# Row maxima of attention scores from 64-row products, neighbours on the lower and the upper half of the rows

## The chip, the core and the metric

The kernel runs on one core of one Trainium2 chip. A core has a matrix engine (TensorE, in the profile PE, its weight loads PEld), three engines for elementwise work (VectorE = DVE, ScalarE = ACT, GpSimd = POOL), a queue engine that issues DMAs (SyncE = SP), an on-chip memory with 128 rows (partitions), and eight banks in which TensorE leaves its results. The metric is the time of one execution on the device in microseconds (us).

## What is computed

A two-layer encoder over 1024 tokens of width 1024: an attention layer and a spatial gating layer, each followed by a squared-ReLU MLP, and a last RMSNorm. The change touches the attention layer alone. It has sixteen query heads of 64 channels. Eight (group A) look at a window of 128 tokens to either side, with one more logit per head; eight (group B) look at all tokens:

```
# group A, banded: s is masked outside |i - j| <= 128
m = jnp.maximum(jnp.max(s, axis=-1, keepdims=True), sink_b)
p = jnp.exp(s - m)
denom = jnp.sum(p, axis=-1, keepdims=True) + jnp.exp(sink_b - m)
# group B
s = jnp.einsum('bqhgd,bkhd->bhgqk', qblk.astype(jnp.float32), kf) * scale
p = jax.nn.softmax(s, axis=-1)
```

The row maximum m only shifts the exponent; any number near it gives the same p / denom. So it can be taken from a coarser product than the scores themselves.

## The kernel before, in words

Most products are made in three parts: each f32 operand is split into a high part, rounded to the format that TensorE takes in one pass (float32r), and a low part, the rest; the products high x high, high x low and low x high are added.

For the scores of a head, rows 0 to 63 and 64 to 127 of the on-chip memory are used for two parts at once. `load_head` brings the queries: R1 (tile r1, in listings r) holds the high part twice, in rows 0 to 63 and again in 64 to 127; R2 (r2) holds the low part in rows 0 to 63, and rows 64 to 127 later take the negated row maxima. `load_k` brings the keys of a key head: k1 holds the high part in rows 0 to 63 and the low part in rows 64 to 127; k2 holds the high part in rows 0 to 63 and ones in rows 64 to 127 (a memset on GpSimd). A score tile (st) is then k1 x R1 + k2 x R2, two products of 128 rows, shifted by the maxima already; group A has a third between them for the mask. ScalarE takes the exponent (pe, ea), and for group B the result is split again (pp, on ScalarE, VectorE and GpSimd) for the products with the values (av).

The maxima come ahead of that, from products of their own (tile mx): R1 x k1, that is q_high x (k_high + k_low), one product of 128 rows. `mx_units` makes the list of them for a head: for group B sixteen, two halves of 512 keys for each of eight blocks of 128 queries; for group A eight, with 256 or 384 keys each. VectorE reduces each to one column (mb for group B, mj and ma with mask and sink for group A). After four query blocks the columns are gathered (m), and `bcast` turns them on TensorE into a row for every partition (bc), which VectorE copies into rows 64 to 127 of R2.

The order around the change: `heads` runs b, b, a, a, b, a, b, a and so on. Each head has 16 units (b) or 8 (a); in a unit come a score tile, then as many mx as `mx_to` asks for, then the av products of the unit six back. `mx_to(count)` issues mx units until `count` of them have been issued in all, so that the maxima run two to two and a half heads ahead. The first ones stand in the last projection, whose products are named lin. A scheduler then lays down the order within each engine, and waits are added from it. All result tiles (st, mx, av, bc, lin) share the eight banks.

Of the kernel before, what the change touches and what calls it, by code (L numbers as in the profile page):

```python
# [13 lines left out]
P = 128  # L14
# [18 lines left out]
def tile_kernel(ctx: ExitStack, tc: tile.TileContext, I, out, upto=99, dbg=None):  # L33
    nc = tc.nc
    pe, act, dve, pool, sp = nc.tensor, nc.scalar, nc.vector, nc.gpsimd, nc.sync
# [11 lines left out]
    def nm(s):  # L47
        uid[0] += 1
        return f"{s}_{uid[0]}"

    def blk(s, dt=F32R):
        return blkp.tile([P, 2, HN], dt, tag="blk", name=nm(s))

    def tr(s, dt=F32):
        return trp.tile([P, HN], dt, tag="tr", name=nm(s))
# [4 lines left out]
    def sm(s, shape):  # L60
        return smp.tile(shape, F32, tag=s, name=nm(s))

    def ps(s):
        return psp.tile([P, HN], F32, tag="ps", name=nm(s))

    def f(ap):
        return ap.bitcast(F32)
# [3 lines left out]
    def mm(o, l, r, start, stop, **kw):  # L71
        last_mm[0] = pe.matmul(o, l, r, start=start, stop=stop, **kw)  # L72
# [396 lines left out]
    for half in range(2):  # L469
# [27 lines left out]
        for tb in range(4):  # L497
            sc = rc[:, tb : tb + 1]
            for kv in range(4):
                src = vp[tb // 2][:, tb % 2, kv * 64 : (kv + 1) * 64]  # L500
                hi = v1[kv][:, half * 4 + tb, 0:64]
# [32 lines left out]
    heads, seen = [], {"a": 0, "b": 0}  # L534
# [3 lines left out]
    k1, k2 = {}, {}  # L538
    R1, R2 = {}, {}
# [3 lines left out]
    def kv_of(hd):  # L543
        return (0 if hd[0] == "a" else 2) + hd[1] // 4

    def load_k(kv):
        a = blk("k1")
        b = blk("k2")
        hi, lo = (qs["k"][part, kv].rearrange("r n t -> (r n) t") for part in range(2))
        sp.dma_start(f(a[0:64].rearrange("p a b -> p (a b)")), hi)  # L550
        sp.dma_start(f(a[64:128].rearrange("p a b -> p (a b)")), lo)
        sp.dma_start(f(b[0:64].rearrange("p a b -> p (a b)")), hi)
        pool.memset(f(b[64:128]), 1.0)
        k1[kv] = a.rearrange("p a b -> p (a b)")
        k2[kv] = b.rearrange("p a b -> p (a b)")

    def load_head(n):
        hd = heads[n]
        kv = kv_of(hd)
        if kv not in k1:  # L560
            load_k(kv)
        key = f"{hd[0]}{hd[1] // 4}"
        assert all((q, half) in ready for q in (key, "k") for half in range(2))
        hi, lo = (qs[key][part, hd[1] % 4].rearrange("r n t -> (r n) t") for part in range(2))
        a, b = blk("r1"), blk("r2")
        a = a.rearrange("p a b -> p (a b)")
        b = b.rearrange("p a b -> p (a b)")
        sp.dma_start(f(a[0:64]), hi)
        sp.dma_start(f(a[64:128]), hi)
        sp.dma_start(f(b[0:64]), lo)  # L570
        R1[n], R2[n] = a, b


    def mx_units(n):
        hd = heads[n]
        kv = kv_of(hd)
        if hd[0] == "a":
            M[n] = sm("ma", [P, 8])

            def unit(tb):  # L580
                lo, hi = max(tb - 1, 0), min(tb + 2, 8)
                w_ = (hi - lo) * P
                off = (lo - tb + 1) * P
                p_ = ps("mx")[:, 0:w_]
                mm(p_, R1[n][:, tb * P : (tb + 1) * P], k1[kv][:, lo * P : hi * P], True, True)
                j = tr("mj")
                dve.tensor_tensor_reduce(
                    j[:, 0:w_], p_, maskq[:, off : off + w_], 1.0, sink8[:, hd[1] : hd[1] + 1],
                    ALU.add, ALU.max, M[n][:, tb : tb + 1],
                )  # L590
                if tb % 4 == 3:
                    m4 = smp.tile([P, 4], F32R, tag="m4", name=nm("m4"))
                    dve.tensor_copy(m4, M[n][:, tb - 3 : tb + 1])
                    chains.append(bcast(n, tb // 4, m4))

            return [lambda tb=tb: unit(tb) for tb in range(8)]
        M[n] = sm("mb", [P, 8, 2])

        def unit(tb, kh):
            p_ = ps("mx")  # L600
            ks = slice(kh * HN, (kh + 1) * HN)
            mm(p_, R1[n][:, tb * P : (tb + 1) * P], k1[kv][:, ks], True, True)
            dve.tensor_reduce(M[n][:, tb, kh : kh + 1], p_, axis=AX.X, op=ALU.max)  # L603
            if tb % 4 == 3 and kh == 1:
                m4 = smp.tile([P, 4], F32R, tag="m4", name=nm("m4"))
                dve.tensor_reduce(m4, M[n][:, tb - 3 : tb + 1, :], axis=AX.X, op=ALU.max)
                chains.append(bcast(n, tb // 4, m4))

        return [lambda tb=tb, kh=kh: unit(tb, kh) for tb in range(8) for kh in range(2)]

    def bcast(n, half, m4):
        for _ in range(2):
            yield 1
        p_ = ps("bc")
        for i in range(4):
            mm(p_[:, i * P : (i + 1) * P], m4[:, i : i + 1].to_broadcast([P, P]), identn, i == 0, i == 3)
        dve.tensor_copy(R2[n][64:128, half * HN : (half + 1) * HN], p_[64:128])
        shifted.add((n, half))
# [141 lines left out]
    def n_mx(n):  # L760
        return sum(8 if hd[0] == "a" else 16 for hd in heads[: max(n, 0)])

    def mx_to(count):

        while mxn[1] < min(count, n_mx(16)):
            if not mxq:
                mxq.extend(mx_units(mxn[0]))
                mxn[0] += 1
            mxq.pop(0)()
            mxn[1] += 1  # L770

    def qa_hook(half, k):
        if half == 1:
            if k == 1:
                load_to(2)
            if k >= 3:
                mx_to((k - 3 + 1) * 4)
# [5 lines left out]
    for n in range(16):  # L783
        if n > 0:
            load_to(n + 3)
        units = st_units(n)
        start, goal = mxn[1], n_mx(n + 2) + int((n_mx(n + 3) - n_mx(n + 2)) * 0.6)
        if n == 0:
            goal = n_mx(2)
        for i, u in enumerate(units):  # L790
            avs = u()
            mx_to(start + -(-(goal - start) * (i + 1) // len(units)))
            avq.append(avs)
            if len(avq) > LAG:
                for a in avq.pop(0):
                    a()
            tick()
        if n >= 13:
            ahead(base[3] + (n - 12))
# [558 lines left out]
```

## Time and profile before

| | |
|---|---|
| median of 3 runs | 2095.03 us (2094.3 to 2097.71) |
| profiled execution | 2097.54 us, its span in the trace 2095.8 us |
| TensorE busy | 2036.0 us, 97% of the span, 9126 products |
| weight loads busy | 1676.2 us, 80% |
| VectorE busy | 1459.8 us, 70% |
| ScalarE busy | 961.2 us, 46% |
| GpSimd busy | 564.0 us, 27% |
| mean granted clock of TensorE | 0.992 |

The span runs from the first to the last instruction of the trace. Products are pipelined: a product's busy time covers that of the next one in part, so its price when others follow is the distance between starts. Shares are means over stages that differ; the change lies in the attention stage, some 290 us of the span.

### The profile page before, as it was taken

Reading aid. Unit: us, or ns where it says so; the run is one execution under the profiler, and the core shown is the slowest. Engines: PE = TensorE matmul, PEld = TensorE weight load, DVE = VectorE, ACT = ScalarE, POOL = GpSimd, SP = SyncE. Lnnn points to the kernel's source line nnn. Section 1 sums busy time; section 2 is a strip of 40 time slices with the busy share of each in tenths; the row PEclk is TensorE's granted clock in tenths of the full one; section 3 lists DMA queues with packets and bytes.
Section 4 is the critical chain, followed back from the end, with each engine's and each line's share of the span. In section 5 each row is a group of like instructions: output and inputs, shape, how many; then the busy total and the mean of one; then the engine's idle time right before and its main releaser. Section 6 shows DMA issues by size and latency. Waiting matters only on the chain. (4 is left out here: it accounts for less than half of the span.)

```text
span 2095.8 us, 27079 instructions
## 1 busy us (share of the span) xinstructions
PE 2036.0 (97%) x9126; PEld 1676.2 (80%) x9126; DVE 1459.8 (70%) x2324; ACT 961.2 (46%) x1768; POOL 564.0 (27%) x437
## 2 busy tenths in 40 slices
PE   8998999999899999999999999999899999999997
PEld 7786877788688888888888888887788888888885
DVE  6878878856786666756696545556866667846975
ACT  5525677773433333435454434433433334544542
POOL 4325466543132222200002126322232223000021
PEclk9999999999999999999999999999999999999998
DMA  4364121134044444768464210432254446855542
GB/s 163 125 195 122 42 65 46 31 111 158 23 165 148 151 156 165 264 204 293 131 220 144 77 57 11 151 107 75 81 174 148 161 151 205 294 218 195 170 140 95
DMA packets 207307, 294.92 MB, mean 141 GB/s; under 512 B 19648, under 2 KB 88768, under 8 KB 207168
## 3 DMA queue, kind: packets, MB, share of 16 engines
q1 hardware_dynamic: 207168, 293.19, 42.5%
q8 instruction: 72, 1.18, 0.2%
q14 instruction: 67, 0.55, 0.1%
HBM read 207.13 MB, written 85.98 MB: 140 GB/s over the span
## 5 line engine op out<-in xcount | busy, mean ns | idle before, releaser
L72 PE MATMUL up<-h,w 128*128 128x512 f32 x1536 | 372.2, 395 | 18.6 <-ACT r L916 9.3
L72 PE MATMUL dy<-w,w 128*128 128x512 f32 x1536 | 364.7, 389 | 0.0
L72 PEld LDWEIGHTS up<-h,w 128*128 128x128 f32 x1536 | 292.9, 191 | 83.1 <-ACT r L916 10.1
L72 PEld LDWEIGHTS dy<-w,w 128*128 128x128 f32 x1536 | 288.3, 188 | 60.3 <-issue 0.5
L314 POOL TENSOR_TENSOR ss<-ss,sq 128x512 f32<-128x512 f32 x66 | 103.4, 1568 | 676.7 <-ACT sq L313 582.1
L72 PE MATMUL up<-w,w 128*128 128x512 f32 x1152 | 277.0, 390 | 0.0
L72 PE MATMUL dx<-w,w 128*128 128x512 f32 x1152 | 276.7, 389 | 0.0
L72 PEld LDWEIGHTS up<-w,w 128*128 128x128 f32 x1152 | 216.4, 188 | 46.0 <-issue 1.0
L72 PEld LDWEIGHTS dx<-w,w 128*128 128x128 f32 x1152 | 216.2, 188 | 44.9
L146 ACT CAST w<-wr 128x512 fp32r<-128x512 f32 x288 | 166.7, 620 | 136.9 <-DVE wr L179 37.3
L147 DVE TENSOR_TENSOR w<-wr,w 128x512 fp32r<-128x512 f32 x288 | 198.1, 699 | 24.2 <-ACT w L146 20.1
L72 PE MATMUL lin<-h,w 128*128 128x512 f32 x768 | 181.3, 393 | 1.1 <-POOL w L123 0.5
L72 PEld LDWEIGHTS lin<-h,w 128*128 128x128 f32 x768 | 143.3, 188 | 33.7 <-issue 2.4
L951 POOL TENSOR_TENSOR t<-ua,ub 128x512 f32<-128x512 f32 x32 | 43.9, 1371 | 459.8 <-ACT ua L898 422.9
L645 POOL TENSOR_TENSOR pp<-pe,pp 128x512 fp32r<-128x512 f32 x107 | 143.4, 1362 | 76.9 <-ACT pp L641 60.4
L147 DVE TENSOR_TENSOR w<-ur,w 128x512 fp32r<-128x512 f32 x224 | 156.0, 707 | 5.8 <-ACT w L146 5.6
L146 ACT CAST w<-ur 128x512 fp32r<-128x512 f32 x224 | 135.8, 620 | 42.3 <-DVE w L147 19.7
L147 DVE TENSOR_TENSOR w<-ws,w 128x512 fp32r<-128x512 f32 x128 | 94.0, 734 | 67.5 <-ACT w L146 67.0
L72 PE MATMUL st<-r,k 128*128 128x512 f32 (+2 forms) x384 | 131.0, 398 | 4.6 <-DVE mb L603 3.6
L146 ACT CAST w<-ws 128x512 fp32r<-128x512 f32 x128 | 79.5, 621 | 110.8 <-DVE ws L226 75.8
L898 ACT ACTIVATE ua<-ua 128x512 f32<-128x512 f32 x64 | 40.4, 633 | 179.0 <-DVE ua L897 179.0
L897 DVE SCALAR_TENSOR_TENSOR ua<-up,rstd 128x512 f32<-128x512 f32 x32 | 22.1, 690 | 139.5 <-PE up L72 139.5
(191 smaller groups left out, 3134.2 us busy)
## 6 DMA issues: line engine op xcount, KB each, us to landing
ur<-ucd SPq DMA_DIRECT2D x224, 256.0 KB, 3.6
wr<-in_w SPq DMA_DIRECT2D x256, 128.0 KB, 2.7
ucd<-t SPq DMA_DIRECT2D x128, 256.0 KB, 2.0
wr<-in_w SPq DMA_DIRECT2D x128, 256.0 KB, 3.5
ucd<-ub SPq DMA_DIRECT2D x64, 256.0 KB, 2.0
x<-in_xT SPq DMA_DIRECT2D x32, 256.0 KB, 4.6
xmd<-x SPq DMA_DIRECT2D x32, 256.0 KB, 2.1
ucd<-ua SPq DMA_DIRECT2D x32, 256.0 KB, 2.0
```

The costliest lines, as they stand in the source:

```text
L72: last_mm[0] = pe.matmul(o, l, r, start=start, stop=stop, **kw)
L146: act.copy(w[:, 0], src)
L147: dve.tensor_tensor(w[:, 1], src, f(w[:, 0]), op=ALU.subtract)
L314: pool.tensor_tensor(sumsq[half][:, 0:w_], sumsq[half][:, 0:w_], t, op=ALU.add)
L645: lo.tensor_tensor(pp[:, 1], e, f(pp[:, 0]), op=ALU.subtract)
L897: dve.scalar_tensor_tensor(dst, src, 0.0, r[half], op0=ALU.max, op1=ALU.mult)
L898: act.activation(dst, dst, AF.Square)
L951: pool.tensor_tensor(t3, ua[:, 1], ub[:, 1], op=ALU.subtract)
```

## The change

Each product for the maxima takes 64 rows in place of 128: q_high x k_high, without k_low. There are two places where it can be made. On rows 0 to 63 it is R1's lower half with k2, and on rows 64 to 127 R1's upper half with k1, for which the two parts of k1 change places. Group B uses the lower half for its first 512 keys and the upper for the second, group A the lower for even query blocks and the upper for odd ones. `mx_to` rounds its count up to an even number, so that products are issued in twos.

```diff
@@ load_k
-        sp.dma_start(f(a[0:64].rearrange("p a b -> p (a b)")), hi)
-        sp.dma_start(f(a[64:128].rearrange("p a b -> p (a b)")), lo)
+        sp.dma_start(f(a[0:64].rearrange("p a b -> p (a b)")), lo)
+        sp.dma_start(f(a[64:128].rearrange("p a b -> p (a b)")), hi)
         sp.dma_start(f(b[0:64].rearrange("p a b -> p (a b)")), hi)
         pool.memset(f(b[64:128]), 1.0)
@@ new
+    def mx_mm(p_, n, rows, tb, ks):
+        rs = slice(64 * rows, 64 * rows + 64)
+        mm(p_, R1[n][rs, tb * P : (tb + 1) * P], (k2, k1)[rows][kv_of(heads[n])][rs, ks], True, True)
+
@@ mx_units, group A
-                mm(p_, R1[n][:, tb * P : (tb + 1) * P], k1[kv][:, lo * P : hi * P], True, True)
+                mx_mm(p_, n, tb % 2, tb, slice(lo * P, hi * P))
@@ mx_units, group B
-            mm(p_, R1[n][:, tb * P : (tb + 1) * P], k1[kv][:, ks], True, True)
+            mx_mm(p_, n, kh, tb, ks)
@@ mx_to
+        count += count % 2
         while mxn[1] < min(count, n_mx(16)):
```

On TensorE, in a head of group B (its scores are st, its query tiles r_423 and r_424 before, r_424 and r_425 after), with the maxima of a later head (query tile r_503): k_221 is k1 and k_222 is k2. Before:

```order
L72 MATMUL st_2499<-r_423_2037,k_221_1336 128x512
L72 MATMUL st_2499<-r_424_2038,k_222_1337 128x512
L72 MATMUL mx_2507<-k_221_1336,r_503_2309 128x512
L72 MATMUL av_2426<-pp_2401,v_3_89 128x512
L72 MATMUL av_2426<-pp_2401,v_4_91 128x512
L72 MATMUL av_2426<-pp_2401,v_3_89 128x512
L72 MATMUL st_2513<-r_423_2037,k_221_1336 128x512
L72 MATMUL st_2513<-r_424_2038,k_222_1337 128x512
L72 MATMUL mx_2521<-k_221_1336,r_503_2309 128x512
L72 MATMUL av_2426<-pp_2420,v_3_89 128x512
```

And after:

```order
L72 MATMUL st_2513<-r_424_2043,k_221_1336 128x512
L72 MATMUL st_2513<-r_425_2044,k_222_1337 128x512
L72 MATMUL mx_2521<-k_222_1337,r_503_2309 128x512
L72 MATMUL mx_2524<-k_221_1336,r_503_2309 128x512
L72 MATMUL av_2426<-pp_2423,v_3_89 128x512
L72 MATMUL av_2426<-pp_2423,v_4_91 128x512
L72 MATMUL av_2426<-pp_2423,v_3_89 128x512
L72 MATMUL st_2532<-r_424_2043,k_221_1336 128x512
L72 MATMUL st_2532<-r_425_2044,k_222_1337 128x512
L72 MATMUL av_2426<-pp_2442,v_3_89 128x512
```

One mx in nearly every unit has become two in every second unit, one on k2 (rows 0 to 63) and one on k1 (rows 64 to 127). Before, the 192 products stood in 158 groups, 131 of them single; now in 97, of which 84 are pairs, three are fours, one is a three and nine are single.

On VectorE, at the end of a half head of the same maxima: mb are the maxima, m the gathered column that bcast on TensorE waits for, r the copy back of its result, pp a cast or a difference for the av products. Before:

```order
L645 TENSOR_TENSOR pp_2476<-pe_2474,pp_2476 128x512
L603 TENSOR_REDUCE mb_2388<-mx_2521 128x1
L643 CAST pp_2504<-pe_2502 128x512
L603 TENSOR_REDUCE mb_2388<-mx_2535 128x1
L606 TENSOR_REDUCE m_575_2538<-mb_2388 128x4
L603 TENSOR_REDUCE mb_2388<-mx_2553 128x1
L617 CAST r_504_2310<-bc_2573 64x512
```

And after (the lines are numbered 5 higher there):

```order
L650 TENSOR_TENSOR pp_2476<-pe_2474,pp_2476 128x512
L608 TENSOR_REDUCE mb_2388<-mx_2521 128x1
L648 CAST pp_2507<-pe_2505 128x512
L608 TENSOR_REDUCE mb_2388<-mx_2524 128x1
L611 TENSOR_REDUCE m_572_2527<-mb_2388 128x4
L608 TENSOR_REDUCE mb_2388<-mx_2553 128x1
L608 TENSOR_REDUCE mb_2388<-mx_2556 128x1
L622 CAST r_504_2310<-bc_2563 64x512
```

Two maxima of the next half, in place of one, now stand between the gathered column and the copy back. The reductions themselves are the same in number and size.

## Rows read from the trace of the kernel before

**Rows 1.** Busy us of PE, PEld, DVE, ACT, POOL (instructions); clock, DMA share, GB/s.

```profile
148.00:437.00 289.00, 271.53 (x1275) 221.52 (x1275) 239.84 (x433) 199.22 (x368) 157.37 (x120) 0.99 0.24 63
```

**Rows 2.** Waits of TensorE from 148 to 437 us: us, times, longest.

```profile
PE bc L72 <- DVE m L606: 4.1, 3, 1.4
PE st L72 <- DVE mb L603: 3.6, 5, 0.9
PE bc L72 <- DVE m L593: 2.5, 3, 1.1
...
PE av L72 <- DVE mb L603: 0.9, 1, 0.9
```

**Rows 3.** The same table as rows 1 by ten us, two stretches.

```profile
300.00:310.00 10.00, 9.23 (x45) 7.61 (x44) 8.85 (x16) 4.60 (x10) 5.74 (x5) 1.00 0.25 61
...
400.00:410.00 10.00, 7.67 (x33) 5.35 (x31) 9.87 (x14) 8.06 (x17) 6.71 (x5) 1.00 0.31 79
```

**Rows 4.** Instructions on tile mx (min/median/max ns), and groups by form (busy, mean ns).

```profile
L72 PEld LDWEIGHTS mx<-k,r x192: 186/188/193, 147.8 to 436.9; 128*128 128x128 f32 x192
L603 DVE TENSOR_REDUCE mb<-mx x128: 673/679/693, 148.5 to 417.6; 128x1 f32<-128x512 f32 x128
L587 DVE CUSTOM_DVE_ANT_0 mj<-mx,maskq,sink x64: 473/616/621, 197.6 to 438.2; 128x384 f32<-128x384 f32 x48, 128x256 f32<-128x256 f32 x16
...
L72 PE MATMUL mx<-k,r 128*128 128x512 f32 x128 | 46.7, 398 | 1.4 <-DVE r L617 0.7 <-DVE mb L603 0.4
L72 PE MATMUL av<-ea,v 128*128 128x384 f32 x64 | 25.4, 485 | 0.0
L72 PE MATMUL mx<-k,r 128*128 128x384 f32 x48 | 16.1, 338 | 0.0
L72 PE MATMUL mx<-k,r 128*128 128x256 f32 x16 | 4.5, 280 | 0.0
```

**Rows 5.** Timeline of TensorE's products in a B head: start, us, what.

```profile
323.16 0.62 PE L72 MATMUL st<-r,k 128*128 128x512 f32 x2
323.63 0.40 PE L72 MATMUL mx<-k,r 128*128 128x512 f32 x1
323.86 0.85 PE L72 MATMUL av<-pp,v 128*128 128x512 f32 x3
324.54 0.61 PE L72 MATMUL st<-r,k 128*128 128x512 f32 x2
```

**Rows 6.** The same timeline in an A head, 384 and 256 columns.

```profile
300.85 0.34 PE L72 MATMUL st<-maskk,identn 128*128 128x384 f32 x1
301.02 0.35 PE L72 MATMUL st<-r,k 128*128 128x384 f32 x1
...
308.00 0.28 PE L72 MATMUL st<-r,k 128*128 128x256 f32 x1
308.12 0.28 PE L72 MATMUL st<-maskk,identn 128*128 128x256 f32 x1
```

**Rows 7.** Timeline of the weight loads at the place of rows 5.

```profile
323.63 0.65 PEld L72 LDWEIGHTS av<-pp,v 128*128 128x128 f32 x3
```

**Rows 8.** An mx product after a wait, on the same timeline.

```profile
406.29 0.50 PE L72 MATMUL mx<-k,r 128*128 128x512 f32 x1
```

**Rows 9.** Timeline: f32 products (av from ea) beside others.

```profile
318.04 0.81 PE L72 MATMUL av<-ea,v 128*128 128x384 f32 x2
318.39 0.91 PE L72 MATMUL st<-r,k 128*128 128x512 f32 x2
319.14 1.03 PE L72 MATMUL av<-ea,v 128*128 128x384 f32 x4
```

**Rows 10.** Issue of the third K DMA, landing times of K, first mx weight load.

```profile
136.90 0.60 SPq L552 DMA_DIRECT2D k<-qs_k  x1
...
DMA to landing us min/median/max: 3.5/4.6/5.6
...
147.83 0.87 PEld L72 LDWEIGHTS mx<-k,r 128*128 128x128 f32 x4
```

## The prediction

> **What bounds the kernel now.** I read the stages first. The products whose maxima are taken, called mx, run from 148 to 437 us [rows 4], and in those 289 us TensorE is busy 271.5, VectorE 239.8, ScalarE 199.2 and GpSimd 157.4 [rows 1]; what follows has no mx. So 17.5 us of the stage are open on TensorE, and all other time there is matrix work back to back. The waits of TensorE in that stage come next. The three longest end with VectorE, and a fourth does: 4.1 + 3.6 + 2.5 + 0.9 = 11.1 us, for the maxima of a half head (m) or for a bank that a maximum (mb) still holds [rows 2]. Third, the shares by ten microseconds: in 15 of the 29 stretches from 150 to 440 us VectorE is at 8.8 of 10 or more, and TensorE idles in such stretches [rows 3]. So TensorE sets the time of nine tenths of the stage and more, with VectorE close behind it. [...]
>
> **What an mx product costs.** There are 192: 128 with 512 columns, 48 with 384, 16 with 256 [rows 4]. Their busy time (398 ns) overlaps the next product's, so the price is the distance of starts. Three av products that follow one another start at 323.86 and the next thing at 324.54, which is 0.227 us for 512 columns [rows 5]. For 384 columns the distance is 0.17 and for 256 it is 0.12 [rows 6]. The weight load of an mx takes 188 ns and lies beneath the product before it: the loads of the three av at 323.63 start with the mx product itself [rows 5, 7].
>
> **The change, part by part.** *The rows.* Each product reads 64 rows where it read 128. Its columns stay, and so do the outputs and the 128 + 64 reductions on VectorE (679 and 616 ns in the median) [rows 4]. A product alone saves nothing, as its time goes by columns. What can be saved is that two neighbours on different halves of the rows, writing to two banks, run at one time. By the order of the changed kernel the 192 products stand in 97 groups between other work: 52 pairs of 512 + 512 columns, three groups of four and one of three (59 such pairs together), 16 pairs of 384 + 384, 16 of 384 + 256, and nine single products.
>
> *The gain, from both sides.* No row shows a product on 64 rows. Below, the pair takes as long as two products, and the gain is nothing. Above, it takes as long as its longer product: 59 x 0.227 + 16 x 0.17 + 16 x 0.12 = 13.4 + 2.7 + 1.9 = 18.0 us. Two weight loads must also fit into the time of one pair. Products of 256 columns, each with a load of its own, start every 0.12 us [rows 6], so a pair can't go below 0.24, and the sum is 59 x 0.21 + 16 x 0.10 + 16 x 0.05 = 12.4 + 1.6 + 0.8 = 14.8. I take 16.5, between the two with overlap: the halves share neither rows nor a bank, and parts of TensorE that don't share anything do overlap in the rows, as the load beneath the product does. [...]
>
> *The switch.* Each of the 97 groups changes from 128 rows to 64 and back, 194 changes, and the trace has none. Below, a change is free. Above, TensorE lets the last product run out and then loads weights in the open. The run-out is 0.40 busy less 0.227, 0.17 us [rows 5]. The load in the open is what the first product after a wait takes more, 0.50 at 406.29 against 0.40: 0.10 us [rows 5, 8]. Together 0.27 a change, 52 us in all. The nearest rows of a change in how the array works are those between products in plain f32 (av from ea) and the others. An f32 product of 384 columns is busy 485 ns against 338 for an mx, so one more stream of columns, 0.15; two of them and two of 512 columns then need 2 x (0.17 + 0.15) + 2 x 0.227 = 1.09, and took 319.14 - 318.04 = 1.10 [rows 4, 9]. That leaves nothing for two changes. I take 0.02 a change, what two such stamps can hide: 3.9 us. The gain on TensorE is 16.5 - 3.9 = 12.6 us. It is gone when a change costs 16.5 / 194 = 0.085.
>
> *What VectorE lets through.* Half of the stretches have VectorE at 8.8 or more. There the stage can't shorten by much more than the 0.1 to 1.2 us of ten that VectorE has free [rows 3], against the 0.4 (12.6 in 289) that TensorE would save; in these I count half, in the others all. So three quarters of 12.6 arrive, 9.5 us.
>
> *Two at a time.* Rounding the count up issues at most one product earlier, never later. Two maxima now come at once, so a cast of pp that VectorE makes behind them is up to 0.68 us later; its av product runs six units after it, and a unit of st, st, mx, av, av, av takes 324.54 - 323.16 = 1.38 us [rows 5], which covers it. Were that cover gone, each such cast would cost the 0.68. The pair needs two free banks of eight at once. Where VectorE is behind, this wait grows: it is 3.6 + 0.9 us now [rows 2], and I leave it there and keep its doubling for a rival.
>
> *The K load.* The products on the lower half now need the third of the three DMAs of a key head, not only the first two. It is issued at 136.90 and a landing takes at most 5.6 us, so 142.5; the first mx loads its weights at 147.83 [rows 10]. For the other heads the query loads come behind it on the same queue, and mx waited for these already. So it costs nothing. Without the 5 us of cover the first pair would stand 0.6 us, the distance of one DMA's issue. Which part of k1 holds the high or the low half changes no sum.
>
> *The sum.* Profiled execution 2097.54 us, span 2095.8 in it: less 9.5 is 2088.0. The profile lies 2.5 above the median of the runs, 2095.03, so there I forecast 2085.5, 0.45% less. About 0.2% (4.2 us) is what a measurement of this kernel tells from no change.
>
> **The rivals.** *The array must run empty at each change* (slower). Place: both edges of each of the 97 groups. Price: 0.27 by the rows above, 52.4 - 16.5 = 36 us more, of which up to 11.1 us fall into the waits for VectorE that are there now: 2120 to 2131. It turns the forecast's sign from 0.085 a change. For it speaks that a load in the open has a price in the rows, and that no row shows a load for 64 rows beneath a product of 128; against it that the f32 change leaves no gap. [...]
> *Only the load stands open*: 0.10 x 194 = 19.4, less 16.5, so 3 us more, 2098, of which the waits may take most: 2095 to 2099.
> *The two halves run one after the other* and a change is free: the change then does not do what it can do, and only the order differs: 2095, give or take 3.
> *VectorE takes the gain*: the bank waits double (4.5 us more) and the 9.5 shrink to 5: 2090.
>
> **How the numbers follow.** I give the forecast 0.40, VectorE taking half 0.07, the open load alone 0.13, one after the other 0.13, the empty array 0.27. Faster by over 0.2%: 0.40 and 0.06 of the 0.07, 0.46. Within 0.2%: 0.12 of one after the other, 0.05 of the open load, 0.01 of VectorE's: 0.18. Slower: 0.27 + 0.08 + 0.01 = 0.36. The forecast's own range is 2077 (all 18.0 arrive) to 2091. For 8 in 10 the range must reach into the empty array, whose price can lie anywhere from 0.15 to 0.27 (2102 to 2131): 2078 to 2122 leaves out its upper third, some 0.10, and 0.05 below.
>
> **What would show it.** In the profile of the changed kernel: the second of a pair should start within some 0.02 to 0.12 us of the first, not 0.227; seven products st, st, mx, mx, av, av, av, which at 0.227 each would take 1.59, should take 1.4; the stage from the first mx to the last should be 9 to 10 us shorter than 289 with VectorE's busy time unchanged near 240, and waits for mb and m longer. If the empty array is right, the weight load before the first mx and the one after the last start only after the product before has ended, with gaps of 0.1 to 0.3 us at both edges and a stage of 315 us or more. If starts within the pair stay at 0.227, the halves don't overlap. Wrong altogether would be a difference that arises outside 148 to 437 us.

## The result and the profile after

The changed kernel takes 2116.43 us in the median of five runs (2114.82 to 2117.81), against 2095.03 before: a ratio of 1.0097, 95% interval 1.0082 to 1.0112. It is 21.4 us slower, where 9.5 us less had been forecast. The runs further down were made on other chips, each beside the kernel before, whose median there was 2095.9 to 2097.3 us; "more than before" is always counted from the kernel before on the same chip, and a ratio is to it. The profiled execution took 2117.58 us, its span 2115.8, which is 20.0 more than the span before.

All of it arises in the attention. The last unit of score products starts at 448.78 us before and at 469.30 after, 20.5 us later, and nothing is added behind it. The stage of the maxima has these sums (columns as in [rows 1]):

```profile
147.00:453.00 306.00, 293.65 (x1261) 204.23 (x1260) 235.57 (x428) 197.64 (x361) 154.19 (x118) 0.96 0.22 58
```

The maxima now run to 452 us, not to 437. VectorE is busy 236 us of 306 in place of 240 of 289, so it is further from being the bound than before. TensorE is busy 22 us longer with products that take 64 rows in place of 128. A part of that is the clock, whose mean fell from 0.99 to 0.96; it is priced in the part on why the prediction was wrong. Its weight loads are busy 17 us less, because the two loads of a pair lie side by side: they take 0.18 us together (below), and 91 pairs at 0.18 make some 16 us. What the products lose shows in the timeline of a B head, at a place like that of [rows 5]:

```profile
331.61 0.62 PE L72 MATMUL st<-r,k 128*128 128x512 f32 x2
332.16 0.50 PE L72 MATMUL mx<-k,r 64*128 64x512 f32 x2
332.59 0.97 PE L72 MATMUL av<-pp,v 128*128 128x512 f32 x3
333.40 0.62 PE L72 MATMUL st<-r,k 128*128 128x512 f32 x2
```

And the weight loads there:

```profile
331.38 0.42 PEld L72 LDWEIGHTS st<-r,k 128*128 128x128 f32 x2
332.16 0.18 PEld L72 LDWEIGHTS mx<-k,r 64*128 64x128 f32 x2 [0.36 <-issue]
332.59 0.53 PEld L72 LDWEIGHTS av<-pp,v 128*128 128x128 f32 x3 [0.25 <-issue]
```

Two things are to be seen. First, the pair overlaps: two products end within 0.50 us, and a single one elsewhere takes the same 0.50 with the same 0.43 to the next thing:

```profile
222.59 0.34 PE L72 MATMUL st<-r,k 128*128 128x384 f32 x1
222.86 0.50 PE L72 MATMUL mx<-k,r 64*128 64x512 f32 x1
223.29 0.95 PE L72 MATMUL av<-pp,v 128*128 128x512 f32 x3
```

Second, both edges cost. The two st should need 2 x 0.227 = 0.45 us; the first mx starts 0.55 after them, 0.10 late. Its weight load starts with it, not beneath the product before, and the mx takes 0.50 where the 128-row product took 0.40 ([rows 5, 8]: what a first product after a wait takes). At the way out it is the same: 0.43 to the next product is 0.20 more than the 0.227 of 512 columns [rows 5], 0.10 of it the longer mx and 0.10 a gap; and the three av take 0.97 where they took 0.85. That is twice a gap of 0.10, and 0.10 and 0.12 for a load that stands open, about 0.42 us for a group (mx products that stand next to one another). From st to st it is 333.40 - 331.61 = 1.79 us for seven products that need 7 x 0.227 = 1.59: a pair costs 0.20 us in place of saving 0.21.

TensorE's waits from 164 us on, in the form of [rows 2] (all the rows there are):

```profile
PE bc L72 <- DVE m L611: 5.5, 2, 4.5
PE av L72 <- DVE mb L608: 3.4, 3, 1.4
PE bc L72 <- ACT pp L646: 2.3, 3, 1.0
PE st L72 <- DVE mb L608: 0.5, 1, 0.5
PE bc L72 <- DVE m L598: 0.3, 1, 0.3
PE mx L72 <- DVE den L685: 0.3, 1, 0.3
```

They sum to 12.3 us. The same table of before, with all its rows, sums to 17.2. So waits for VectorE are not what grew in sum, though a single one did: 4.5 us for the maxima of the first heads.

The theory after the result: TensorE runs out and loads weights in the open at each of the 194 changes between 128 and 64 rows. Its rival: the order in twos is what costs, with two maxima at once on VectorE and two banks at once. A second question is whether the overlap is worth anything in the end.

### The profile page after: what moved, and what is told of

Its sections match the earlier page's. It is cut to its first block, busy times and chain, and to the rows that moved or that the text cites. A ratio compares the mean times of both kernels' runs of the same rounds, so it can differ in the third digit from the quotient of the medians.

```text
span 2115.8 us, 27099 instructions
## 1 busy us (share of the span) xinstructions
PE 2062.6 (97%) x9126; PEld 1662.1 (79%) x9126; DVE 1459.9 (69%) x2324; ACT 963.8 (46%) x1768; POOL 563.4 (27%) x437
## 5 line engine op out<-in xcount | busy, mean ns | idle before, releaser
L72 PE MATMUL av<-pp,v 128*128 128x512 f32 x384 | 116.3, 414 | 3.4 <-DVE mb L608 3.4
```

## The experiments

**Order alone, and rows alone.** Three kernels take the change apart. The first has the rounding of the count without the 64 rows:

```diff
     def mx_to(count):
+        count += count % 2
```

> The kernel before with one line of the change: the count of maxima products is rounded up to even, so they are issued in twos, still on 128 rows and with both parts of k. If the loss of the change lies in the switches between products of 128 and of 64 rows, this kernel takes what the one before takes, 2095 us, give or take 3. If it lies in the order (two maxima at once fill the banks and VectorE falls behind), it takes most of the 21 us: 2110 to 2117.

Measured: 2101.97 us, ratio 1.0026 (1.0016 to 1.0035). So the order in twos costs 5.4 us by the ratio (4.7 by the two medians), a quarter of the loss: more than the theory had (0 to 3) and far less than the rival. TensorE's waits grow from 17.2 to 19.0 us; they grow where the first heads start, at 177 us, and at three places where av waits behind two maxima:

```profile
PE bc L72 <- DVE m L606: 6.9, 2, 5.8
PE av L72 <- DVE mb L603: 4.3, 3, 1.4
PE bc L72 <- ACT pp L641: 2.5, 3, 1.0
```

The other 3 us or so go with a lower clock, which is taken up in the part on why the prediction was wrong.

The second keeps everything of the change but puts all products on the lower half (`mx_mm(p_, n, 0, ...)` in both places).

> The changed kernel with all maxima products on the lower half of the rows (k2), none on the upper, so that no two can run at one time; the twos stay. If the halves do overlap in the changed kernel and the two switches of each group cost what the trace shows, the overlap that is lost is worth 91 pairs, 15 to 18 us: 2131 to 2135. If the overlap is worth nothing in the end, because something else sets the pace, it stays at 2116.

Measured: 2127.06 us, ratio 1.0140 (1.0123 to 1.0157), 29.8 us more than before, where the changed kernel takes 21.4 more. So the overlap is worth 8.4 us of time (10.6 if the two medians are compared as they stand), less than the expected 15 to 18. What else differs between the two runs can account for the rest. This one waits 10.7 us where the changed kernel waits 12.3, and it works less at the lower clock: by the estimate given further down that costs it 5.1 us, and the changed kernel 10.9. With these 1.6 and 5.8 us added the overlap is worth 15.8 us, an estimate too.

The third takes the rounding out of the changed kernel again, which leaves the halves in turn, but mostly one by one.

> The changed kernel without the rounding: halves in turn, but in the order of the kernel before, with 159 groups (133 of them single products) in place of 97. If each group costs two switches of about 0.21 us: 159 x 0.43 = 68 us less some 5 for the pairs that are left, of which up to 11 us lie in waits for VectorE: 2147 to 2158. If the order in twos is what costs, this is faster than the changed kernel: 2095 to 2105.

Measured: 2135.38 us, ratio 1.0182 (1.0167 to 1.0197). The order is that of the kernel before, and it is the slowest of the three: the rival falls. It is nearly 12 us below the lower edge of what was expected. The whole table of TensorE's waits shows part of why:

```profile
PE av L72 <- DVE mb L608: 0.9, 1, 0.9
PE av L72 <- POOL pp L650: 0.7, 1, 0.7
PE st L72 <- DVE w L428: 0.6, 1, 0.6
PE bc L72 <- DVE m L598: 0.6, 1, 0.6
PE st L72 <- DVE mb L608: 0.5, 1, 0.5
PE av L72 <- DVE pp L648: 0.2, 1, 0.2
```

3.5 us are left of 17.2: where TensorE itself is slower, it no longer waits for VectorE.

**The price by itself.** In the attention, other engines answer to every change. In the down projection of the first MLP they don't: TensorE's products dy and dx follow one another with no idle time at all, in 112 steps of twelve products; in all four kernels compared here TensorE is busy in 380.0 of the 380 us from 750 to 1130, at a granted clock of 1.00. There one product of a step is put on the lower 64 rows, then also its neighbour, on the other half or the same one. Halves of these products are left out.

```diff
                 for m in range(4):
-                    mm3(acc[m], w, u, slice(m * P, (m + 1) * P), ...)
+                    # ra: rows of acc[1]'s first product, rc: rows of acc[0]'s last; else all 128
+                    mm(acc[m], w[ra, 0, ls], u[ra, 0], ...)
+                    mm(acc[m], w[:, 0, ls], u[:, 1], ...)
+                    mm(acc[m], w[rc, 1, ls], u[rc, 0], ...)
```

> The disputed price by itself, where nothing else waits: the kernel before, with its attention as it was, but in the down projection of the first MLP one of the twelve products of each of the 112 steps takes only the lower 64 rows (the other half of that product is left out, so the output is not the reference's). Two changes of row count per step, no second half to overlap. From the changed kernel's trace a single group costs about 0.40 us: 112 x 0.40 = 45 us more, 2140. If the loss in the attention is one of banks and VectorE and a change as such is cheap (0.02), it is 4 us more at most.

> The same, but the next product of the step, into another bank, takes only the upper 64 rows (halves of both products left out). Two changes per step as in the one before, and a pair that can overlap: 0.40 less one product's 0.227, so 112 x 0.18 = 20 us more than before, 2116. If two halves do not overlap, the same as with one product: 45 more.

> The same with both products on the lower 64 rows (halves of both left out): two changes per step, no overlap. 45 us more than before, 2140, if it is the two halves that bring the overlap; 20 more if any two 64-row products overlap.

| 64-row products in a step | median, us | ratio (95%) | more per step, us |
|---|---|---|---|
| one | 2140.34 | 1.0215 (1.0200 to 1.0230) | 0.40 |
| two, lower and upper half | 2117.01 | 1.0106 (1.0091 to 1.0121) | 0.19 |
| two, both on the lower half | 2143.34 | 1.0231 (1.0216 to 1.0246) | 0.42 |

The last column is the difference to 2095.9, the median before on that chip, over 112. All three came out as expected, to 3 us. The trace shows it step by step. Starts of two successive steps in the kernel before:

```profile
863.66 2.88 PE L72 MATMUL dx<-w,w 128*128 128x512 f32 x12
866.38 2.88 PE L72 MATMUL dy<-w,w 128*128 128x512 f32 x12
```

With one 64-row product:

```profile
862.41 3.28 PE L72 MATMUL dx<-w,w 128*128 128x512 f32 x12
865.53 3.28 PE L72 MATMUL dy<-w,w 128*128 128x512 f32 x12
```

With one on each half:

```profile
861.79 3.08 PE L72 MATMUL dx<-w,w 128*128 128x512 f32 x12
864.71 3.09 PE L72 MATMUL dy<-w,w 128*128 128x512 f32 x12
```

With two on the lower half:

```profile
863.28 3.31 PE L72 MATMUL dx<-w,w 128*128 128x512 f32 x12
866.42 3.31 PE L72 MATMUL dy<-w,w 128*128 128x512 f32 x12
```

2.72, 3.12, 2.92 and 3.14 us from step to step. (The rows give the shape of a group's first product; the 64-row ones are inside.) Two changes of row count cost 0.40 us, with no other engine in play. A neighbour on the other half, into another bank, takes 0.20 of its 0.227 us off again. A second 64-row product on the same half leaves the step at 3.14 against 3.12, so the price hangs on the change and not on the number of such products. The weight loads of a step with one 64-row product have the two gaps that the attention has:

```profile
900.39 0.18 PEld L72 LDWEIGHTS dx<-w,w 64*128 64x128 f32 x1 [0.35 <-issue]
900.82 1.89 PEld L72 LDWEIGHTS dx<-w,w 128*128 128x128 f32 x9 [0.24 <-issue]
```

**Fewer changes.** If a group costs 0.40 and a pair gives 0.21 back (0.40 less 0.19 in the table), two pairs in a group about break even, and more should gain. The count is rounded up to a multiple of four products, so most groups are two pairs:

```diff
-        count += count % 2
+        count = -(-count // 4) * 4
```

> The changed kernel with the count rounded up to a multiple of four: 55 groups, most of four products, halves in turn. By the switches: 55 x 0.43 = 24 us less 18 for the overlap, so 2101, and up to 10 more where four maxima at once wait for banks: 2099 to 2111. If the bursts on VectorE are what costs, it is slower than the changed kernel: over 2116.

> The kernel before with the maxima products issued in fours, on 128 rows and with both parts of k. The run in fours on 64 rows took 2111; by the switches 55 groups cost 55 x 0.42 = 23 us and the overlap gives 18 back, so the order in fours as such should cost the other 9: 2104 to 2108. If the order in fours costs nothing (2095 to 2099), the price of a group of four on 64 rows is larger than the trace's 0.42.

Measured: 2111.16 us on 64 rows, ratio 1.0067 (1.0052 to 1.0082), and 2107.31 on 128 rows, ratio 1.0059 (1.0042 to 1.0076). Both lie where expected (the first at its upper edge). The order in fours costs 11.4 us, and 64 rows add 2.5 to that (13.9 less 11.4; 3.9 if the two medians are compared as they stand), which is no more than the two intervals leave open. In twos they add 16.7 (21.4 less 4.7), one by one 38.1. So the loss does shrink as the changes get fewer, down to about break-even; a gain is not seen. The price of the order stands in good part in the waits, which sum to 25.2 us on 128 rows against 17.2 before:

```profile
PE bc L72 <- DVE m L606: 12.4, 10, 4.0
PE mx L72 <- DVE den L680: 6.2, 3, 2.5
PE bc L72 <- DVE m L593: 2.7, 3, 1.2
```

bc waits for a gathered maximum that now stands behind four reductions, and mx waits for a bank that VectorE has yet to read (den is its read of a finished av).

With eights in place of fours:

> The changed kernel with the count rounded up to a multiple of eight: 35 groups on 64 rows. By the price of the steps in the MLP (0.40 us a group, 0.21 back for each pair): 35 x 0.40 = 14 us less 91 x 0.2 = 18, so 4 us less than the same order on 128 rows. In time: the order in eights on 128 rows (its own run) less 0 to 6. If the price of a group grows with its size, it is slower than that run.

> The kernel before with the maxima products issued in eights on 128 rows. Twos cost 5 us and fours 11 by their runs, so eights 12 to 25 us: 2108 to 2121, in waits for VectorE. If the order's cost does not grow with the burst, 2107 as in fours.

Measured: 2160.80 us on 64 rows, ratio 1.0307 (1.0289 to 1.0324), and 2149.30 on 128, ratio 1.0254 (1.0239 to 1.0270). Both miss. The order in eights costs 53 us, more than twice what had been expected, and 64 rows cost 11.5 us where they should have given 4 back. In the sums of the stage the clock stands out, first 64 rows, then 128 (columns as in [rows 1]):

```profile
148.00:500.00 352.00, 310.17 (x1263) 228.42 (x1262) 234.12 (x435) 195.06 (x362) 156.34 (x118) 0.90 0.20 51
```

```profile
148.00:500.00 352.00, 311.67 (x1342) 241.85 (x1341) 243.16 (x444) 207.91 (x386) 168.75 (x126) 0.95 0.22 57
```

A granted clock of 0.90 in place of 0.95 over 352 us is 18 us of full speed, more than the 11.5 to be explained. The waits hardly differ: 39.9 us in the whole table on 64 rows and 38.8 on 128. What 64 rows as such do in eights can't be told from this pair of runs.

No version tried beats the kernel before.

## Why the prediction was wrong

**The step that failed** is *the switch*: 0.02 us a change was taken between bounds of 0 and 0.27, and it is 0.20 (0.40 a step for two in the MLP). The break-even of 0.085 that the text gives was right, and 0.20 lies far on the other side. Nearest was taken to be the change between plain f32 and the other format, which leaves no gap in [rows 9] (1.10 us, 1.09 added up); that row says nothing of row counts. At 0.20 a change a group of one pair costs more than the pair gives back, so the forecast had the sign wrong: 2116.4 lies within its range of 2078 to 2122 only because that had been stretched for the rival below. The rows that did hold the price were those of the upper bound: 0.10 for a load in the open [rows 8] was measured as 0.11 (0.10 on the mx and 0.12 on the av; in the MLP a 64-row product is busy 498 ns and most 128-row ones 389), and the run-out, bounded by 0.17 [rows 5], as 0.10 (0.55 less 0.45).

**The rival that came true** is the array that must run empty at each change. It had 0.27 of the chances and a price of 2120 to 2131. The two parts of its price are in the trace, 0.10 us of gap and 0.11 of load at each edge, and the price was too high: 0.20 a change and not 0.27, 2116.4 us, and a stage of 305 us (147.4 to 452.2) where its sign was to be 315 or more. That the array is empty at the change is not shown: in the timeline the last st before the pair is busy to 332.23, and the load for the pair starts at 332.16. [rows 5, 7] have the load beneath the product before, which holds for products of one row count: after the change, too, the loads of the two st start at 331.38 and the st at 331.61. It was wrong to let that count, silently, for a load that follows a product of another row count; there it starts with its own product, at 332.16 and at 332.59.

**The gain** was right in mechanism and size. Neighbours on two halves overlap almost wholly, 0.20 of 0.227 us in a step of the MLP. 59 pairs at 0.21, 16 of 384 + 384 at 0.155 (208.74 - 207.02 = 1.72 us for a unit that needs 1.48, so 0.245 of the 0.40 is left) and 16 of 384 + 256 at some 0.1 make 16.5, the number taken. In time it came to 8.4 us by the run on one half, and to an estimated 15.8 once waits and clock are allowed for.

**Two at a time** was costed at nothing and costs some 5 us. The cover of six units for pp holds (no av waits for a pp in that run), but the waits for m and for banks, which the text left as they were, grew: the waits for m from 6.6 to 8.7 us and those behind mb from 4.9 to 6.3 in the run on 128 rows, all waits together by 1.8. The rival that doubled the bank waits had nearly this price (4.5), but by luck: the bank waits did not double, and the larger part of the price goes with the clock.

**The clock** has no term in the forecast's sum; it was 0.99 over the stage [rows 1]. It would have needed one. In the changed kernel the granted clock is 0.50 from 168.3 to 182.0, from 345.8 to 352.6 and from 424.3 to 431.1 us, 27 us in all, against 3.4 us before (lines in the last section). Three av products take 1.28 us to the next start there (348.36 to 349.64), against 0.68 at a clock of 1.00 [rows 5]. TensorE is busy in some 22 of the 27 us; if the same work at 1.00 takes half of that, the lower clock costs about 10.9 us, and 1.6 before; counted in the same way it is 4.6 in the order in twos on 128 rows, 5.1 on one half and 1.5 one by one. These are estimates from the busy time in stretches of one us; some of it can be hidden by waits. The five runs of the changed kernel point the same way: the two with a mean granted clock of 0.990 took 2114.8 and 2115.4 us, the two with 0.987 took 2117.6 and 2117.8. The second and the third stretch begin while TensorE sits in the second of two waits close together, 1.4 us of av behind a pair of maxima and 1.0 us of bc for pp. The run in twos on 128 rows goes down to 0.50 right behind the same two waits, from 340.1 to 343.5 us; the run one by one has no such pair of waits (its whole table stands above) and no such stretch. Why the first stretch begins at 168.3 us, with TensorE busy in nearly all of the eight us before, is not shown.

**What VectorE lets through** had the right direction for the other sign as well. Three quarters of a gain were to arrive; of a loss, part falls into the waits that are there: one by one, 17.2 us of them shrink to 3.5.

The sum, with the measured terms: 97 groups x 0.40 = 38.8, less 16.5 for the overlap, is 22.3. TensorE's waits go from 17.2 to 12.3, which takes 4.9 off, and the clock adds 10.9 less 1.6, 9.3: 26.7, where 21.4 were measured. For the run one by one it is 159 x 0.40 less 5.5, less 13.7 of waits, 44.4, with the clock as before, where 38.1 were measured; for the run on one half 38.8, less 6.5 of waits, and 3.5 of clock, 35.8, where 29.8 were measured. All three come out 5 to 6 us too high. Either a group costs 0.34 to 0.36 us on the mean in the attention and not the 0.40 of the MLP, or a part is hidden in a way that neither the waits nor the clock show; that stays open.

The K load cost nothing, as forecast: the first mx starts at 147.41, against 148.06 before.

## What to carry to other kernels

Two half-height products on different rows do run at one time, but the change into and out of half height costs twice 0.2 us here, nearly as much as two products of 512 columns (0.45). By these prices two pairs in a row break even and only longer rows of pairs can gain, where the engines behind can take them in a burst; no run here showed a gain. So count the changes before the pairs. An order that comes in bursts makes waits (25.2 us in fours on 128 rows, 17.2 before), and here a lower clock came with them (0.95 over the stage in eights on 128 rows, 0.99 before), so the clock of every stage belongs in the sum of the result. And when a trace has no row for a mechanism, take the bound that is made of the parts it would need (a run-out, a load in the open), not the row that merely looks alike.

## What was not expected of the hardware

The pair's overlap is all but complete: two products of 512 columns on two halves take 0.50 us from the first start to the last end, and one alone takes 0.50. With both on one half, a step of the MLP takes 3.14 us against 2.92, 0.22 more, close to the 0.227 of one product [rows 5]: there they run one after the other.

The clock fell lower where the products come in bursts. In the stage of the maxima it was 0.99 before, 0.96 after the change, and 0.90 in eights on 64 rows against 0.95 in eights on 128; one by one on 64 rows it was 0.99. Before, it goes down once, in the first of these lines. After the change the deepest place is the stretch that follows the start of the first heads (second line), where TensorE is busy 5.5 us of ten while it waits for the first heads' maxima and the clock is at 0.50 all along; the third and the fourth line hold the two places behind a pair.

```profile
180.00:190.00 10.00, 10.00 (x41) 8.27 (x40) 9.14 (x14) 6.78 (x13) 4.39 (x4) 0.86 1.04 263
```

```profile
170.00:180.00 10.00, 5.54 (x15) 3.17 (x14) 9.90 (x16) 5.90 (x12) 2.66 (x3) 0.50 0.13 50
340.00:350.00 10.00, 7.53 (x28) 5.50 (x27) 8.81 (x13) 7.99 (x16) 8.00 (x7) 0.79 0.31 81
420.00:430.00 10.00, 7.54 (x25) 5.09 (x24) 8.29 (x12) 6.65 (x13) 8.00 (x7) 0.72 0.00 1
```
